# The memory values' panel first, the keys scaled as they are evicted, twelve zero products

## The chip, the cores and the metric

The kernel runs on one core of a Trainium2 chip. The metric is the time of one execution on the device, in microseconds. Of the core's engines, TensorE (PE in the profile) multiplies, VectorE (DVE) and ScalarE (ACT) work element by element and empty the accumulators, GpSimd (POOL) only sets a few constants, and SyncE (SP) issues nearly all transfers.

## What is computed

A trunk of two layers over 256 tokens of width 2048. Layer 0 mixes with gated linear attention, layer 1 with forgetting attention; each layer also attends with 4 heads to 256 memory tokens, and each ends in a gated MLP with a short convolution. The change touches how the memory's keys and values come about. The reference for that part:

```python
def memory_kv(mem_n, w_kv):
    mk, mv = split_cols(mem_n @ w_kv, [MEM_WIDTH, MEM_WIDTH])
    return split_heads(mk, MEM_HEADS), split_heads(mv, MEM_HEADS)
...
    mem_n = rmsnorm(mem, norm_mem)
...
    for i in range(DEPTH):
...
        mk, mv = memory_kv(mem_n, mem_w_kv[i])
```

MEM_WIDTH is 512: keys and values of a layer are 256 tokens by 512 columns, from weights of 2048 rows. rmsnorm divides each token by the root of the mean of its squares and multiplies by a gain for each of the 2048 columns.

## The kernel before

All weights are one stream (`wp`), laid out by `_panels` (L55) in the order in which they are used. A panel is one group of output columns over all 16 chunks of 128 rows. It is cut into units of 512 KB, 128 x 1024 numbers: four chunks of 256 columns, or two chunks of 512.

Every product is made from parts, to keep float32 accuracy. `load_unit` and `split_unit` (L187 to L211) load a unit into `raw` (four buffers), cast it on ScalarE to its high part `whi` (three buffers, L201) and subtract on VectorE to get its low part `wlo` (L210). They run at a raised priority, up to 300 instructions ahead of where they stand. `split` (L302 to L310) does the same to a chunk of activations: the high half of a buffer is cast with the gain on ScalarE (L309), the low half computed on VectorE (L310). `bufA` and `bufB` hold 16 such chunks each.

There are two kinds of panel:

- `proj_fm` (L213) leaves the output with its columns on the partitions. The weights are the stationary side, the activations (high and low side by side, 512 columns) the moving one: for each chunk and each of two accumulators a product of 512 columns with `whi` (L235) and one of 256 with `wlo` (L236). A panel has 4 units. `whole` (L240) adds an accumulator's two halves.
- `proj_tm` (L248) leaves the tokens on the partitions. The activations are stationary, the weights (up to 512 columns) move: for each chunk and each of two blocks of tokens three products (L272 to L274). A panel has 8 units of two chunks; in each unit block 0 goes first.

Both take two of the four accumulators (`acc`, pool `pacc`) for a panel and empty them when the panel is over, with the function `evac` that they are given.

The start of the run goes like this. Eight zero products (`WARM`, L177 and L178) of 128 x 512 keep TensorE busy from a cleared buffer. Then come two keys' panels of layer 0 (`("mk", 0, j)`, 256 columns each, `proj_fm`), its values' panel (`("mv", 0)`, 512 columns, `proj_tm`), and the same three for layer 1. The memory itself comes in during the first panel: `take_mem` (L431) is called ahead of each half of a unit, issues the transfers of `memt` (first tile in two pieces, one on ScalarE's queue, then a tile of 512 KB for each unit) and splits two chunks into `bufA`. The transfers of `gains`, `mask`, `xf` (the input, 16 pieces) and `x` are issued on SP's queue between those of the weights; `tc.issue_after` holds them behind a named instruction.

The memory's norm (`Norm`, L312, here `nrm`) isn't applied to the activations, only the gain is; the factor of each token is applied to the outputs. In `first_out` (L466), after the first panel, four squares are taken (L473) and added up (L475 to L477). `mean` (L329) sums over the partitions with small products against ones (L334); `col` (L347) makes the factor of each token as a column on the partitions, with Newton steps on VectorE (L342 to L345); `row` (L358) turns it into a row with two more products (L370) and a copy (L373). The values take the column as they are evicted (`mv_out`, L464). The keys of layer 0 are evicted without the norm (L453, L454) and all four tiles of them are multiplied by the row when the second panel is over (L457); those of layer 1 are multiplied by the row as they are evicted (L459).

The order of the instructions on each engine is set when the kernel is built, by a scheduler that goes by priorities and by its own estimate of when each is ready; each engine then runs its list in order. The scheduler isn't changed.

Of the kernel before, what the change touches and what calls it, by code (L numbers as in the profile page):

```python
# [12 lines left out]
F32 = mybir.dt.float32  # L13
# [6 lines left out]
P = 128  # L20
# [18 lines left out]
AHEAD = 300  # L39

OG_EARLY = 2
WARM = 8

FV_PARTS = ((0, 376), (376, 764), (764, 1152), (1152, 1536))

# [9 lines left out]
def _panels():  # L55

    full = list(range(KC))
    out = []  # L60

    def fm(key, w, c0, kcs=full, second=None):
        cols = [(c0, 256)] if second is None else [(c0, 128), (second, 128)]
        out.append((key, w, kcs, cols, 4))

    def tm(key, w, c0, n, kcs=full, more=()):
        out.append((key, w, kcs, [(c0, n), *more], 2))

    for l in range(2):
        for j in range(2):  # L70
            fm(("mk", l, j), ("mem_w_kv", l), j * 256)
        tm(("mv", l), ("mem_w_kv", l), 512, 512)
    tm(("gv", 0), ("gla_w_in", 0), G_V, DV, more=[(G_R, RANK)])
    for j in range(2):
        fm(("mq", 0, j), ("gla_w_in", 0), G_MQ + j * 256)
    for h in range(GLA_H):
        fm(("gq", h), ("gla_w_in", 0), G_Q + h * DK)
        fm(("gk", h), ("gla_w_in", 0), G_K + h * DK)
        for j in range(OG_EARLY if h == GLA_H - 1 else 0):
            fm(("og", j), ("gla_w_in", 0), G_OG + j * 256)  # L80
# [12 lines left out]

    for f in range(4):
        tm(("wo", 0, f), ("gla_w_out", 0), f * 512, 512, late)
    ffn(0)
    for j in range(6):
        fm(("fk", j), ("fox_w_kv", None), F_K + j * 256)
    for j, (lo, hi) in enumerate(FV_PARTS):
        more = [] if j else [(F_L, FOX_H)]  # L100
        tm(("fv", j), ("fox_w_kv", None), F_V + lo, hi - lo, more=more)
    for j in range(2):
        fm(("mq", 1, j), ("fox_w_in", 0), FOX_H * HD + j * 256)
    for j in range(6):
        fm(("fq", j), ("fox_w_in", 0), j * 256)
    for f in range(4):
        tm(("wo", 1, f), ("fox_w_out", 0), f * 512, 512, late)
    ffn(1)
    return out
# [29 lines left out]
def _trunk(ctx: ExitStack, tc: tile.TileContext, xt, xtok, memt, wp, wgu, gns, gfin, cnv, par, msk, out):  # L139
# [70 lines left out]
                V.tensor_tensor(lo[:, s], raw[:, s], hi[:, s].bitcast(F32), ALU.subtract)  # L210
        return hi, lo  # L211

    def proj_fm(key, src, evac, before=None):  # L213

        units = where[key]
        total = sum(len(u[1]) for u in units)
        acc = [pacc.tile([P, 512], F32, name="acc", tag="acc") for _ in range(2)]
        base = min(min(u[1]) for u in units)
        done = 0
        for n, unit in enumerate(units):  # L220
            if before is None:
                hi, lo = split_unit(unit)
            else:
                hi, lo = split_unit(unit, 2, lambda half: before(n, half), whole=n > 0)
            for j, kc in enumerate(unit[1]):
                for c in range(2):
                    product(acc[c], c, total - 1, done, src[kc - base], hi, lo, j)
                done += 1
        for c in range(2):
            evac(c, acc[c])  # L230
# [14 lines left out]
        V.tensor_tensor(r, a[:, :T], t, ALU.add)  # L245
        return r

    def proj_tm(key, src, evac, spare=None):  # L248

        units = where[key]
        n = units[0][2]
        base = min(min(u[1]) for u in units)
        acc = [pacc.tile([P, 512], F32, name="acc", tag="acc") for _ in range(2)]
        ahead = 0 if spare is None else 4
        ready = {}
        for i in range(len(units) + ahead):
            for b, u in ((0, i), (1, i - ahead)):
                if not 0 <= u < len(units):  # L260
                    continue
                if b == 0:
                    ready[u] = split_unit(units[u], pool=wpool if spare is None or u < 3 else spare)
                hi, lo = ready[u]
                kcs = units[u][1]
                a = acc[b][:, :n]
                xs = slice(b * P, (b + 1) * P)
                for j, kc in enumerate(kcs):
                    s = slice(j * n, (j + 1) * n)
                    xk = src[kc - base]  # L270
                    last = u == len(units) - 1 and j == len(kcs) - 1
                    TE.matmul(a, xk[:, 0, xs], hi[:, s], start=u == 0 and j == 0, stop=False)  # L272
                    TE.matmul(a, xk[:, 0, xs], lo[:, s], start=False, stop=False)  # L273
                    TE.matmul(a, xk[:, 1, xs], hi[:, s], start=False, stop=last)  # L274
                if u == len(units) - 1:
                    evac(b, a)
# [150 lines left out]
    with tc.tile_pool(name="load", bufs=1) as lp:  # L427
        mraw = [lp.tile([P, KC + 4 * T], F32, name=f"mt{i}") for i in range(4)]
        mt = [t[:, KC:].rearrange("p (c t) -> p c t", t=T) for t in mraw]

        def take_mem(g, half):  # L431

            if g == 0:
                s = slice(half * (KC + 2 * T), KC + (half + 1) * 2 * T)
                (nc.sync if half else nc.scalar).dma_start(mraw[0][:, s], memt[0, :, s])
                if half == 0:
                    S.preload_act_table_set("natural_log_exp_and_others")
                chunks = range(2 * half, 2 * half + 2)
            else:
                if half == 0:  # L440
                    nc.sync.dma_start(mraw[g][:, KC:], memt[g, :, KC:])
                    if g == 1:
                        nc.sync.dma_start(gains, gns)
                chunks = range(2 * half, 2 * half + 2)
            for i in chunks:
                k = 4 * g + i
                split(bufA, k, mt[g][:, i, :], mraw[0][:, k : k + 1])

        def mk_out(l, j):
            def evac(c, a):  # L450
                o = mk[l][:, 2 * j + c, :]
                if l == 0:
                    S.activation(o, a[:, T:], AF.Copy)  # L453
                    V.tensor_tensor(o, o, a[:, :T], ALU.add)  # L454
                    if c == 1 and j == 1:
                        for f in range(MEM_H):
                            V.tensor_tensor(mk[0][:, f, :], mk[0][:, f, :], nrm.row(), ALU.mult)  # L457
                else:
                    V.tensor_tensor(o, whole(a), nrm.row(), ALU.mult)  # L459

            return evac

        def mv_out(l):
            return lambda b, a: S.activation(mv[l][:, b, :], a, AF.Copy, scale=nrm.col()[:, b : b + 1])  # L464

        def first_out(c, a):  # L466
            mk_out(0, 0)(c, a)
            if c == 1:
                nc.sync.dma_start(mask[:, :M_FOX], msk[:, :M_FOX])
                sq, acc = [lp.tile([P, 4, T], F32, name=n) for n in ("sq4", "ssq4")]  # L470
                with tc.issue_after(casts[-1].ins):
                    for g in range(4):
                        S.activation(sq if g else acc, mt[g], AF.Square)  # L473
                        if g:
                            V.tensor_tensor(acc, acc, sq, ALU.add)  # L475
                V.tensor_tensor(acc[:, :2, :], acc[:, :2, :], acc[:, 2:, :], ALU.add)
                V.tensor_tensor(acc[:, 0, :], acc[:, 0, :], acc[:, 1, :], ALU.add)  # L477
                nrm.acc = acc[:, 0, :]

        proj_fm(("mk", 0, 0), bufA, first_out, before=take_mem)  # L480
        proj_fm(("mk", 0, 1), bufA, mk_out(0, 1))
        xf = [lp.tile([P, T], F32, name=f"xf{i}") for i in range(KC)]
        with tc.issue_after(loads[-1].ins):
            for i in range(KC):
                nc.sync.dma_start(xf[i], xt[i])
            nc.sync.dma_start(part, par)
            nc.sync.dma_start(mask[:, M_FOX:], msk[:, M_FOX:])
        proj_tm(("mv", 0), bufA, mv_out(0))
        for i in range(KC):
            split(bufB, i, xf[i], gain("mix0", i))  # L490
        for j in range(2):
            proj_fm(("mk", 1, j), bufA, mk_out(1, j))
            if j == 0:
                with tc.issue_after(loads[-1].ins):
                    for f in range(4):
                        nc.sync.dma_start(x[f], xtok[f])
                for f in range(4):
                    for b in range(2):
                        nx.add(f, b)
        proj_tm(("mv", 1), bufA, mv_out(1))  # L500


# [482 lines left out]
```

## Time and profile before

| | |
|---|---|
| median of 3 runs | 2298.16 us (2298.02 to 2298.43) |
| the profiled execution's own time | 2298.03 us |
| its span in the trace | 2296.2 us |
| TensorE busy | 2284.1 us |
| VectorE busy | 1619.1 us |
| ScalarE busy | 1253.6 us |
| granted TensorE clock, mean | 0.999 |

The span runs from the first to the last recorded instruction; 1.83 us of the execution lie outside it. A row of the timeline has the start and the length in microseconds, the engine, the line of the kernel, the operation, what is written and read with its shape, how many instructions were merged, and in brackets how long the engine was idle before and what ended that. Products on TensorE are pipelined: their lengths overlap, and the distance between starts is what each one costs. A row of the waits has who waited for whom, the total in microseconds, the times, and the longest. A row of the stretches has the borders, the length, then busy time and instructions of PE, its weight loads (PEld), DVE, ACT and POOL, the granted clock, the share of the transfers' engines, and GB/s. A row of the transfers has what is loaded, the queue, the count, the size and the median time from issue to landing. A row of a tile's view has the shortest, the median and the longest in nanoseconds, the first and last start, and the shape.

### The profile page before, as it was taken

The page shows a single profiled execution, that of the slowest core. Times are in us where ns is not written, and L with a number is a line of the kernel's source. Part 1 is how long each engine was busy: PE and PEld are TensorE (multiplying, and loading weights), DVE is VectorE, ACT ScalarE, POOL GpSimd, SP SyncE. Part 2 cuts the span into 40 slices and gives each one's busy share as a digit, 9 for nine tenths or more (in the row PEclk, how much of TensorE's full clock was granted, in tenths as well). Part 3 has the DMA queues.
Part 4 walks back from the last instruction along what each step waited for, and adds up shares of the span by engine and source line. Part 5 has one row for each costly group of instructions (what it writes and reads, how often), then busy time and mean ns, then how long its engine had stood idle before and what let it go on. Part 6 is the DMA issues. An engine that isn't in the chain of part 4 may idle for free.

```text
span 2296.2 us, 33165 instructions
## 1 busy us (share of the span) xinstructions
PE 2284.1 (99%) x12384; PEld 1976.2 (86%) x12384; DVE 1619.1 (71%) x2667; ACT 1253.6 (55%) x1967; POOL 3.1 (0%) x20
## 2 busy tenths in 40 slices
PE   9999999999999999999999999999999999999998
PEld 7889888888888888888888998888888888888886
DVE  7578987577765777557767557657776577756775
ACT  7555555555553555445565455556554455534554
POOL 0000000000000000000000000000000000000000
PEclk9999999999999999999999999999999999999999
DMA  8655455555555555555555664555555555665554
GB/s 320 196 162 161 156 164 179 187 184 189 190 189 194 188 191 187 193 192 191 186 183 187 182 194 152 170 193 184 188 189 192 192 191 186 191 193 192 185 192 156
DMA packets 124745, 430.15 MB, mean 187 GB/s; under 512 B 14108, under 2 KB 18600, under 8 KB 124456
## 3 DMA queue, kind: packets, MB, share of 16 engines
q1 hardware_dynamic: 124152, 427.24, 57.3%
q8 instruction: 97, 1.59, 0.3%
q10 hardware_dynamic: 432, 0.79, 0.1%
q14 instruction: 64, 0.52, 0.1%
HBM read 425.87 MB, written 2.11 MB: 186 GB/s over the span
## 4 chain that ended last, share of the span: by engine, by line
PE 99%; DMA 0%; DVE 0%; ACT 0%; issue 0%; DVEq 0%; ACTq 0%; SPq 0%
PE acc L235 37%; PE acc L236 20%; PE acc L273 12%; PE acc L274 12%; PE acc L272 12%; PE acc L238 2%; PE ps_s L842 0%; PE ps_s L631 0%; PE ps_t L402 0%; PE ps_s L409 0%; PE ps_o L420 0%; PE ps_s L756 0%; PE ps_o L772 0%; PE ps_o L650 0%; DMA raw<-wp 0%; DMA cb<-cdram 0%
## 5 line engine op out<-in xcount | busy, mean ns | idle before, releaser
L210 DVE TENSOR_TENSOR wlo<-raw,whi 128x1024 fp32r<-128x1024 f32 (+4 forms) x812 | 972.8, 1199 | 542.3 <-ACT whi L201 531.3
L201 ACT ACTIVATE whi<-raw 128x1024 fp32r<-128x1024 f32 (+4 forms) x812 | 843.5, 1040 | 778.4 <-PE acc L274 373.7
L235 PE MATMUL acc<-B,whi 128*128 128x512 f32 x1980 | 683.6, 395 | 0.0
L235 PE MATMUL acc<-A,whi 128*128 128x512 f32 x1680 | 580.9, 397 | 1.3 <-DVE A L310 1.3
L236 PE MATMUL acc<-B,wlo 128*128 128x256 f32 x2112 | 550.0, 281 | 0.0
L236 PE MATMUL acc<-A,wlo 128*128 128x256 f32 x1792 | 464.0, 281 | 0.0
L235 PEld LDWEIGHTS acc<-B,whi 128*128 128x128 f32 x1980 | 360.7, 188 | 68.5
L236 PEld LDWEIGHTS acc<-B,wlo 128*128 128x128 f32 x2112 | 397.4, 188 | 21.9
L235 PEld LDWEIGHTS acc<-A,whi 128*128 128x128 f32 x1680 | 305.7, 188 | 58.7 <-DVE A L310 2.0
L236 PEld LDWEIGHTS acc<-A,wlo 128*128 128x128 f32 x1792 | 338.3, 189 | 20.2
L273 PE MATMUL acc<-wlo,B 128*128 128x512 f32 (+3 forms) x736 | 274.8, 374 | 0.9 <-DVE wlo L210 0.9
L274 PE MATMUL acc<-whi,B 128*128 128x512 f32 (+3 forms) x736 | 273.6, 372 | 0.0
L272 PE MATMUL acc<-whi,B 128*128 128x512 f32 (+3 forms) x736 | 247.2, 372 | 0.0
L273 PE MATMUL acc<-wlo,A 128*128 128x512 f32 x544 | 212.3, 390 | 0.0
L274 PE MATMUL acc<-whi,A 128*128 128x512 f32 x544 | 211.8, 389 | 0.0
L272 PE MATMUL acc<-whi,A 128*128 128x512 f32 x544 | 192.4, 390 | 0.0
L243 ACT ACTIVATE part<-acc 128x256 f32<-128x256 f32 x240 | 89.9, 375 | 156.7 <-PE acc L238 156.6
L273 PEld LDWEIGHTS acc<-wlo,B 128*128 128x128 f32 x736 | 138.2, 188 | 20.5 <-DVE wlo L210 1.2
L274 PEld LDWEIGHTS acc<-whi,B 128*128 128x128 f32 x736 | 138.2, 188 | 18.6
L272 PEld LDWEIGHTS acc<-whi,B 128*128 128x128 f32 x736 | 137.3, 188 | 18.7
L245 DVE TENSOR_TENSOR wholes<-acc,part 128x256 f32<-128x256 f32 x240 | 101.2, 422 | 64.2 <-ACT part L243 63.9
L274 PEld LDWEIGHTS acc<-whi,A 128*128 128x128 f32 x544 | 102.2, 188 | 21.1
(213 smaller groups left out, 1578.5 us busy)
## 6 DMA issues: line engine op xcount, KB each, us to landing
raw<-wp SPq DMA_DIRECT2D x743, 512.0 KB, 3.4
raw<-wp SPq DMA_DIRECT2D x32, 384.0 KB, 3.1
raw<-wp SPq DMA_DIRECT2D x24, 388.0 KB, 3.1
raw<-wp SPq DMA_DIRECT2D x8, 400.0 KB, 3.1
xf<-xt SPq DMA_DIRECT2D x16, 128.0 KB, 4.4
x<-xtok SPq DMA_DIRECT2D x4, 512.0 KB, 7.5
mt<-memt SPq DMA_DIRECT2D x3, 512.0 KB, 6.8
cb<-cdram SPq DMA_DIRECT2D x12, 128.0 KB, 3.2
```

What stands on the lines that cost most here:

```text
L201: casts.append(S.activation(hi[:, s], raw[:, s], AF.Copy))
L210: V.tensor_tensor(lo[:, s], raw[:, s], hi[:, s].bitcast(F32), ALU.subtract)
L235: TE.matmul(a, hi[:, s], both, start=done == 0, stop=False)
L236: TE.matmul(a[:, :T], lo[:, s], both[:, 0, :], start=False, stop=False)
L238: TE.matmul(a, hi[:, s], both, start=False, stop=True)
L243: S.activation(t, a[:, T:], AF.Copy)
L245: V.tensor_tensor(r, a[:, :T], t, ALU.add)
L272: TE.matmul(a, xk[:, 0, xs], hi[:, s], start=u == 0 and j == 0, stop=False)
L273: TE.matmul(a, xk[:, 0, xs], lo[:, s], start=False, stop=False)
L274: TE.matmul(a, xk[:, 1, xs], hi[:, s], start=False, stop=last)
```

## The change

Layer 0's values' panel is laid out and computed first, its two keys' panels follow; layer 1 keeps its order. `take_mem` now serves `proj_tm`: each unit takes two chunks, and a 512 KB tile of the memory is fetched with every second unit. The squares are taken one tile at a time inside that panel, the last at its end; the norm's column is made for the values' eviction at the end of the first panel, and the row for the keys' eviction, which now multiplies as layer 1's does. The transfers of `mask` and `gains` are issued after the first panel's last load, those of `xf` after the first keys' panel's last load. The zero products are twelve.

```diff
-WARM = 8
+WARM = 12
...
     for l in range(2):
+        if l == 0:
+            tm(("mv", l), ("mem_w_kv", l), 512, 512)
         for j in range(2):
             fm(("mk", l, j), ("mem_w_kv", l), j * 256)
-        tm(("mv", l), ("mem_w_kv", l), 512, 512)
+        if l:
+            tm(("mv", l), ("mem_w_kv", l), 512, 512)
...
-    def proj_tm(key, src, evac, spare=None):
+    def proj_tm(key, src, evac, spare=None, before=None):
...
-                    ready[u] = split_unit(units[u], pool=wpool if spare is None or u < 3 else spare)
+                    pool = wpool if spare is None or u < 3 else spare
+                    if before is None:
+                        ready[u] = split_unit(units[u], pool=pool)
+                    else:
+                        ready[u] = split_unit(units[u], 2, lambda half: before(u, half), pool, whole=u > 0)
...
+        def take_mem(u, half):
+
+            if half == 0:
+                if u == 0:
+                    nc.scalar.dma_start(mraw[0][:, :n0], memt[0, :, :n0])
                     S.preload_act_table_set("natural_log_exp_and_others")
+                elif u == 1:
+                    nc.sync.dma_start(mraw[0][:, n0:], memt[0, :, n0:])
+                elif u % 2 == 0:
+                    nc.sync.dma_start(mraw[u // 2][:, KC:], memt[u // 2, :, KC:])
+            k = 2 * u + half
+            split(bufA, k, mt[k // 4][:, k % 4, :], mraw[0][:, k : k + 1])
+            if half and u in (3, 5, 7):
+                square(u // 2 - 1)
+
+        n0 = KC + 2 * T
+        sq, ssq = [lp.tile([P, 4, T], F32, name=n) for n in ("sq4", "ssq4")]
+
+        def square(g):
+            S.activation(sq if g else ssq, mt[g], AF.Square)
+            if g:
+                V.tensor_tensor(ssq, ssq, sq, ALU.add)
 
         def mk_out(l, j):
             def evac(c, a):
                 o = mk[l][:, 2 * j + c, :]
-                if l == 0:
-                    S.activation(o, a[:, T:], AF.Copy)
-                    V.tensor_tensor(o, o, a[:, :T], ALU.add)
-                    if c == 1 and j == 1:
-                        for f in range(MEM_H):
-                            V.tensor_tensor(mk[0][:, f, :], mk[0][:, f, :], nrm.row(), ALU.mult)
-                else:
-                    V.tensor_tensor(o, whole(a), nrm.row(), ALU.mult)
+                V.tensor_tensor(o, whole(a), nrm.row(), ALU.mult)
...
+        def first_out(b, a):
+            if b == 0:
+                square(3)
+                V.tensor_tensor(ssq[:, :2, :], ssq[:, :2, :], ssq[:, 2:, :], ALU.add)
+                V.tensor_tensor(ssq[:, 0, :], ssq[:, 0, :], ssq[:, 1, :], ALU.add)
+                nrm.acc = ssq[:, 0, :]
+                with tc.issue_after(loads[-1].ins):
+                    nc.sync.dma_start(mask[:, :M_FOX], msk[:, :M_FOX])
+                    nc.sync.dma_start(gains, gns)
+            mv_out(0)(b, a)
+
+        proj_tm(("mv", 0), bufA, first_out, before=take_mem)
         xf = [lp.tile([P, T], F32, name=f"xf{i}") for i in range(KC)]
...
+        for l in range(2):
+            for j in range(2):
+                proj_fm(("mk", l, j), bufA, mk_out(l, j))
+                if l == j == 0:
+                    with tc.issue_after(loads[-1].ins):
+                        for i in range(KC):
+                            nc.sync.dma_start(xf[i], xt[i])
+                        nc.sync.dma_start(part, par)
+                        nc.sync.dma_start(mask[:, M_FOX:], msk[:, M_FOX:])
+                elif j == 0:
+                    with tc.issue_after(loads[-1].ins):
+                        for f in range(4):
+                            nc.sync.dma_start(x[f], xtok[f])
                     for f in range(4):
-                        nc.sync.dma_start(x[f], xtok[f])
...
+                        for b in range(2):
+                            nx.add(f, b)
+            if l == 0:
+                for i in range(KC):
+                    split(bufB, i, xf[i], gain("mix0", i))
         proj_tm(("mv", 1), bufA, mv_out(1))
```

More of the change, by code (lines that the diff above doesn't have):

```diff
@@ L211, in split_unit, with proj_fm @@
         return hi, lo
-    def proj_fm(key, src, evac, before=None):
+    def proj_fm(key, src, evac):
         units = where[key]
@@ L220, in proj_fm @@
         for n, unit in enumerate(units):
-            if before is None:
-                hi, lo = split_unit(unit)
-            else:
-                hi, lo = split_unit(unit, 2, lambda half: before(n, half), whole=n > 0)
+            hi, lo = split_unit(unit)
             for j, kc in enumerate(unit[1]):
@@ L429, in _trunk @@
         mt = [t[:, KC:].rearrange("p (c t) -> p c t", t=T) for t in mraw]
[L431 to L436, printed above, removed]
-                    S.preload_act_table_set("natural_log_exp_and_others")
[L438 to L447, printed above, removed]
+        def take_mem(u, half):
+            if half == 0:
+                if u == 0:
+                    nc.scalar.dma_start(mraw[0][:, :n0], memt[0, :, :n0])
+                    S.preload_act_table_set("natural_log_exp_and_others")
+                elif u == 1:
[12 more added lines that the diff above has]
+                V.tensor_tensor(ssq, ssq, sq, ALU.add)
         def mk_out(l, j):
@@ L451, in evac @@
                 o = mk[l][:, 2 * j + c, :]
-                if l == 0:
-                    S.activation(o, a[:, T:], AF.Copy)
-                    V.tensor_tensor(o, o, a[:, :T], ALU.add)
-                    if c == 1 and j == 1:
-                        for f in range(MEM_H):
-                            V.tensor_tensor(mk[0][:, f, :], mk[0][:, f, :], nrm.row(), ALU.mult)
-                else:
-                    V.tensor_tensor(o, whole(a), nrm.row(), ALU.mult)
+                V.tensor_tensor(o, whole(a), nrm.row(), ALU.mult)
             return evac
@@ L464, in mv_out @@
             return lambda b, a: S.activation(mv[l][:, b, :], a, AF.Copy, scale=nrm.col()[:, b : b + 1])
[L466 to L478, printed above, removed]
@@ L480, in _trunk @@
-        proj_fm(("mk", 0, 0), bufA, first_out, before=take_mem)
-        proj_fm(("mk", 0, 1), bufA, mk_out(0, 1))
-        xf = [lp.tile([P, T], F32, name=f"xf{i}") for i in range(KC)]
[L483 to L494, printed above, removed]
-                    for f in range(4):
-                        nc.sync.dma_start(x[f], xtok[f])
-                for f in range(4):
-                    for b in range(2):
-                        nx.add(f, b)
+        def first_out(b, a):
[8 more added lines that the diff above has]
+            mv_out(0)(b, a)
```

## The prediction

> **What bounds the kernel now.** I began with the page, then the waits of TensorE, then the first 60 us of the timeline, engine by engine, because only there does the change move anything.
>
> ```profile
> span 2296.2 us, 33165 instructions
> ...
> PE 2284.1 (99%) x12384; PEld 1976.2 (86%) x12384; DVE 1619.1 (71%) x2667; ACT 1253.6 (55%) x1967; POOL 3.1 (0%) x20
> ...
> PE 99%; DMA 0%; DVE 0%; ACT 0%; issue 0%; DVEq 0%; ACTq 0%; SPq 0%
> ```
>
> ```profile
> PE ps_o L178 <- DVE B L175: 1.4, 1, 1.4
> PE acc L235 <- DVE A L310: 1.3, 1, 1.3
> PE acc L273 <- DVE wlo L210: 0.9, 1, 0.9
> ```
>
> TensorE (PE) is the bound from its first instruction to the last product. In the whole span it waits three times: 1.4 us before the zero products, 1.3 us between them and the first real product, 0.9 us once much later. The change keeps every real product, so PE's work has a floor that it cannot lower. What can move is the start, and any wait that the new order brings in.
>
> ```profile
> 1.45 3.78 PE L178 MATMUL ps_o<-B 128*128 128x512 f32 x8 [1.45 <-DVE B L175]
> 6.54 0.80 PE L235 MATMUL acc<-A,whi 128*128 128x512 f32 x1 [1.32 <-DVE A L310]
> ...
> 7.78 0.41 PE L236 MATMUL acc<-A,wlo 128*128 128x256 f32 x1
> ...
> 8.42 0.41 PE L236 MATMUL acc<-A,wlo 128*128 128x256 f32 x1
> ...
> 9.70 0.53 PE L235 MATMUL acc<-A,whi 128*128 128x512 f32 x1
> 10.07 0.40 PE L236 MATMUL acc<-A,wlo 128*128 128x256 f32 x2
> ...
> 10.54 0.28 PE L236 MATMUL acc<-A,wlo 128*128 128x256 f32 x1
> ...
> 10.89 0.27 PE L236 MATMUL acc<-A,wlo 128*128 128x256 f32 x1
> ...
> 19.44 0.63 PE L235 MATMUL acc<-A,whi 128*128 128x512 f32 x2
> ...
> 30.68 0.62 PE L272 MATMUL acc<-whi,A 128*128 128x512 f32 x2
> ...
> 33.41 0.62 PE L272 MATMUL acc<-whi,A 128*128 128x512 f32 x2
> ```
>
> These are starts and lengths on PE. A pair of a 512- and a 256-column product comes every 0.64 us at first (7.78 to 8.42) and every 0.35 us later (10.54 to 10.89); the step between the paces lies between 9.70 and 10.07, say 9.9 us, 3.4 us after the real work began. So 512 columns cost 0.64 x 512/768 = 0.427 us at the slow pace. The first keys' panel takes 19.44 - 6.54 = 12.90 us, the second, with the same products, 30.68 - 19.44 = 11.24 us. The slow pace costs 1.66 us. That sum is the most a better warm-up can return, apart from an earlier start.
>
> **The change, part by part.** Zero products: 12 instead of 8. At 0.427 us each PE is free for other work at 1.45 + 12 x 0.427 = 6.57 us if the pace stays slow until then. (Eight by this working are free at 4.87; the row ends at 5.23 because it includes the last one's way through the array.) Today the real work starts at 6.54, so the four additional ones fill the hole of 1.32 us and delay the start by 0.03 us. What is new is that PE is busy without a break from 1.45 us on.
>
> When the pace rises is the one unknown. In the trace a busy stretch of 3.78 us and a hole did not raise it, and a second stretch raised it after 3.4 us. If 3.4 us of unbroken work are what is wanted, the earliest time is 1.45 + 3.4 = 4.85. With the same reading and the same rhythm as in the trace (steps possible at 9.9, 6.5 and 3.1 us) it rises at 6.5, just as the zero products end. I take 6.5: all of the 1.66 us is then saved. At 4.85, eight zero products are through, and four more at 0.23 us end at 5.8: the real work could start 0.7 us earlier too. At the other end the gain from the pace is nil.
>
> The Trainium skill, page "TensorE: Matmul & The Clock Gate", section "Part 1: The HAM clock gate", says that PE starts at half rate and goes to full rate after a free-running window of about 3.4 us in which it was busy, the window's phase being different from run to run. By that rule the step falls somewhere between 4.9 and 8.3 us here, and the saving between 0.8 and 2.4 us. The trace's 3.4 us and its two paces agree; that eight products failed in one profile fits a window that began before them. The same rule speaks against counting on an exact figure.
>
> The values' panel first: can the first products be fed? The rows are landings of DMAs, two issues on SP's queue, the rate of one stretch, then ScalarE (ACT) and VectorE (DVE).
>
> ```profile
> raw<-wp SPq DMA_DIRECT2D x2, 256.0 KB, 4.2
> mt<-memt ACTq DMA_DIRECT2D x1, 264.0 KB, 4.2
> ...
> 1.18 0.42 SPq L435 DMA_DIRECT2D mt<-memt  x1
> 1.65 0.42 SPq L198 DMA_DIRECT2D raw<-wp  x1
> ...
> 5.00:10.00 5.00, 3.68 (x11) 2.98 (x11) 4.60 (x11) 5.00 (x12) 0.00 (x0) 1.00 1.04 419
> ```
>
> ```profile
> 4.74 0.63 ACT L201 ACTIVATE whi<-raw 128x512 fp32r<-128x512 f32 x1 [2.29 <-DMA raw<-wp]
> 5.27 1.69 ACT L309 ACTIVATE A<-mt 128x256 fp32r<-128x256 f32 x4
> ...
> 8.99 1.14 ACT L201 ACTIVATE whi<-raw 128x512 fp32r<-128x512 f32 x2
> 10.03 1.71 ACT L309 ACTIVATE A<-mt,mt 128x256 fp32r<-128x256 f32 x4
> ...
> 5.40 0.69 DVE L210 TENSOR_TENSOR wlo<-raw,whi 128x512 fp32r<-128x512 f32 x1 [4.01 <-ACT whi L201]
> 6.01 1.67 DVE L310 SCALAR_TENSOR_TENSOR A<-mt,A 128x256 fp32r<-128x256 f32 x4
> 9.78 1.29 DVE L210 TENSOR_TENSOR wlo<-raw,whi 128x512 fp32r<-128x512 f32 x2
> 10.98 1.67 DVE L310 SCALAR_TENSOR_TENSOR A<-mt,mt,A 128x256 fp32r<-128x256 f32 x4
> ```
>
> One unit of weights (512 KB) feeds PE for 33.41 - 30.68 = 2.73 us in the values' panel and 8 x 0.35 = 2.8 us in a keys' panel, but it asks for two chunks of the memory instead of four. ACT then needs 1.04 + 2 x 0.40 = 1.84 us a unit where it now needs 2.65, DVE 1.20 + 2 x 0.40 = 2.0 instead of 2.8. So today both engines run exactly as fast as PE in the first panel; afterwards they have 0.7 to 0.9 us a unit to spare. That matters because PE at full pace asks for unit 1 earlier than now.
>
> The transfers: up to unit 2 they are 264 + 3 x 256 + 3 x 512 = 2568 KB; 520 KB of it is there at 4.74, the rest follows at 419 GB/s in 2.10 MB / 0.419 = 5.0 us, at 9.75 us. PE wants unit 2 at 6.57 + 2 x 2.73 = 12.0; a half cast, a chunk's split and the low parts take 0.63 + 0.49 + 0.69 + 0.48 = 2.3 us in a row, so it is met even then. Unit 1 (1544 KB, 7.2 us, wanted at 9.3) is as safe, and units 3 to 7 need 1024 and 512 KB in turn per 2.73 us. The second half of unit 0 is the closest: the half lands near 5.9 at the latest (issued at 1.65 as now, + 4.2; in the new order it takes the place at 1.18), its cast follows by 6.5 and its low part by 7.3, and PE wants them at 6.57 + 3 x 0.23 = 7.3. I cost that at 0, bounded by 0.4 us. A first product that no longer spans a chunk's high and low half can go at 5.27 + 0.49 = 5.8; with 12 zero products at slow pace that gives nothing.
>
> The norm of the memory and the evictions:
>
> ```profile
> 15.32 1.04 ACT L473 ACTIVATE ssq<-mt 128x1024 f32<-128x1024 f32 x1
> ...
> 17.35 1.22 DVE L475 TENSOR_TENSOR ssq<-ssq,sq 128x1024 f32<-128x1024 f32 x1 [0.71 <-ACT sq L473]
> ...
> 34.71 0.42 DVE L477 TENSOR_TENSOR ssq<-ssq 128x256 f32<-128x256 f32 x1
> 36.59 0.61 PE L334 MATMUL ps_t<-mask,ssq 128*128 128x128 f32 x4
> ...
> 45.51 0.16 DVE L345 TENSOR_TENSOR ny<-ny,nt 128x2 f32<-128x2 f32 x1
> ...
> 51.98 0.69 ACT L464 ACTIVATE mv<-acc,ny 128x512 f32<-128x512 f32 x1 [0.53 <-PE acc L274]
> 54.58 0.36 ACT L373 ACTIVATE row<-ps_t 128x256 f32<-128x256 f32 x1
> L457 DVE TENSOR_TENSOR mk<-mk,row x4: 418/418/426, 55.0 to 56.0; 128x256 f32<-128x256 f32 x4
> L459 DVE TENSOR_TENSOR mk<-wholes,row x4: 424/424/427, 66.1 to 78.5; 128x256 f32<-128x256 f32 x4
> ```
>
> Four multiplications of 0.418 us go and four of 0.424 come, and copies and additions keep their number: nothing on PE. The four squares (1.04 us) and three additions (1.22 us) move forward into the first panel, into the spare time above: three squares are 3 us against 8 x 0.9 = 7 us on ACT. The DMAs of mask and gains move behind the eight units' weights on SP's queue; the first use of the mask is the product of L334. The 16 of xf move to behind the first keys' panel, still two panels into the run; what is made of them is read only after layer 1's three memory panels.
>
> New is a wait. There are four accumulators. Values' and first keys' panel take them all; the second keys' panel needs those of the values, whose eviction needs the column ny, and layer 1's keys need those of the first, whose eviction needs the row. In the new order the values end at 6.57 + 8 x 2.73 = 28.4, the first keys at 28.4 + 11.24 = 39.7, the second at 50.9. The column comes today 45.67 - 34.71 = 11.0 us after the start of the last addition, the row 20.2 us after it. The last square needs the last memory transfer (with the weights ahead of it 5128 KB: 4.74 + 4.72 MB / 0.419 = 16 us, later if the weights' buffers hold it back); then ACT's spare time sets it near 20 to 22, DVE's last addition near 25. Column at 36, eviction at 37; row at 45, evictions at 47. Both are 3 to 4 us ahead of need. Behind a late eviction stand ACT's and DVE's casts of the next units. Price 0, if the last addition starts by 28.
>
> Sum against the profiled execution: 2298.03 us, of which 1.83 lie outside its span; +0.03 - 1.66 + 0 = 2296.4. The runs' median is 2298.16, 0.13 above that execution, so 2296.5 us.
>
> **Rivals.** First, the pace rises later. If it takes 3.4 us of slow zero work plus 3.4 us of slow real work, counted together from 1.45, it rises near 1.45 + 3.8 + 3.4 = 8.6; 2.0 us at slow pace after 6.57 cost 1.0, the gain is 0.6, the time 2297.5. For it: eight products were not enough. Against: a hole lay in between.
>
> Second, the change doesn't do what it says: products of zeros do not count, and the pace rises 3.4 us after the real start, at 9.97. Then the cost is today's plus 0.03: 2298.2. For it: 3.78 us of them had no visible effect.
>
> Third, slower: the late column. If the last square queues on ACT behind the casts until the values' panel is over, it ends at 29.4, the additions (1.22, 0.69, 0.42) with a unit's low part between them (1.22) start their last by 32.6, the column comes at 43.6, the eviction ends at 44.3, and PE stands from 39.7 on: 4.6 us, and up to 1.66 again if a hole of that length brings the slow pace of the start back. 2298.16 - 1.63 + 4.6 + 1.66 = 2302.8. It decides as soon as the last addition starts after 28. For it: today the chain is loose, 11 and 20 us for a few small operations. Against: ACT has spare time before 28, and nothing else wants it.
>
> **How the numbers follow.** Forecast 0.68, later rise 0.14, no effect 0.08, late column 0.10 (half of it a partial stall of 1 to 3 us, so 2297.5 to 2299.5). The forecast's own range is 2295.8 (pace up at 4.85) to 2297.4 (up one step of 3.4 us after that, at 8.3, so (8.3 - 6.57)/2 = 0.9 us lost). The range runs from 2295.2, with 0.5 us for an earlier start than the sum allows, to 2299.0, which takes in the two mild rivals and most partial stalls. About 0.2%, 4.6 us, is what a measurement tells from no change: faster by that 0.02 (nothing found could give it), slower 0.04 (the full late column, or a stall that I do not see), within it 0.94.
>
> **What would show it.** Right: twelve zero products from 1.45 us, no hole of a microsecond after them, pairs of products 0.23 us apart from the first or second unit on, no wait of PE on an accumulator near 40 or 51 us, and the start of layer 1's keys 1.6 us earlier than today. Wrong: 0.427 us a product beyond 9 us (the first two rivals), a wait on a low part or a chunk in the first 15 us (the feed was mis-sized), or idle PE near 40 us with the eviction of the values behind it (the third).

## The result, and the profile after

| | median of 11 runs | range | ratio to before (95%) |
|---|---|---|---|
| before | 2298.16 us | 2298.01 to 2298.73 | |
| after | 2303.95 us | 2301.80 to 2305.68 | 1.0025 [1.0017, 1.0032] |

The change makes the kernel slower by 5.8 us, where a gain of 1.7 us was forecast. The executions also scatter: over 3.9 us, where those of the kernel before scatter over 0.7. The profiled execution of after is the fastest of the eleven (2301.80 us, span 2299.7). A second execution is shown among the experiments.

The page of the kernel after, and its waits of TensorE. In the code after, L181 is the line of the zero products, L204 and L213 make a unit's high and low part, L276 to L278 are the three products of a values' panel, L313 and L314 split a chunk, L454 and L456 are the squares and their additions, L466 evicts the values.

```profile
span 2299.7 us, 33177 instructions
...
PE 2285.0 (99%) x12388; PEld 1976.1 (86%) x12388; DVE 1618.6 (70%) x2671; ACT 1253.9 (55%) x1971; POOL 3.1 (0%) x20
```

```profile
PE acc L277 <- DVE wlo L213: 2.4, 3, 0.9
PE acc L235 <- DVE wholes L245: 2.1, 1, 2.1
PE ps_o L181 <- DVE B L178: 1.4, 1, 1.4
PE acc L276 <- ACT whi L204: 0.2, 1, 0.2
```

TensorE's busy time is nearly what it was. New are a wait of 2.1 us for `wholes`, which is the emptying of a keys' accumulator, and waits for casts and low parts (of the three for low parts one comes late in the run and was there before, too). The timeline of TensorE after, at the places that matter:

```profile
1.45 5.36 PE L181 MATMUL ps_o<-B 128*128 128x512 f32 x12 [1.45 <-DVE B L178]
6.65 0.62 PE L276 MATMUL acc<-whi,A 128*128 128x512 f32 x2
...
12.52 0.73 PE L276 MATMUL acc<-whi,A 128*128 128x512 f32 x2 [0.23 <-ACT whi L204]
13.87 0.50 PE L277 MATMUL acc<-wlo,A 128*128 128x512 f32 x1 [0.61 <-DVE wlo L213]
...
20.57 0.50 PE L277 MATMUL acc<-wlo,A 128*128 128x512 f32 x1 [0.93 <-DVE wlo L213]
...
31.16 0.40 PE L235 MATMUL acc<-A,whi 128*128 128x512 f32 x1
...
45.16 0.50 PE L235 MATMUL acc<-A,whi 128*128 128x512 f32 x1 [2.13 <-DVE wholes L245]
...
56.80 0.62 PE L235 MATMUL acc<-A,whi 128*128 128x512 f32 x2
```

The panels begin at 6.65 (values), 31.16 (first keys), 45.16 (second keys) and 56.80 us (layer 1's keys). The last point was reached at 53.17 us before. That is 3.6 us later, and the span grew by 3.5: all of the loss lies ahead of this point, and what follows is unchanged. The values' panel took 24.51 us instead of 8 x 2.73 = 21.8: 2.7 us lost. The first keys' panel and the hole behind it took 14.00 us, where the panel alone needs 11.24 and the norm's small products 0.4: 2.4 us lost. The two losses, less the 1.66 us of the slow pace that are gone, come to 3.4 us.

Who stood ahead? The timelines of ScalarE and VectorE after:

```profile
7.31 1.04 ACT L454 ACTIVATE ssq<-mt 128x1024 f32<-128x1024 f32 x1
8.26 1.14 ACT L204 ACTIVATE whi<-raw 128x512 fp32r<-128x512 f32 x2
...
10.90 1.05 ACT L454 ACTIVATE sq<-mt 128x1024 f32<-128x1024 f32 x1
11.86 2.17 ACT L204 ACTIVATE whi<-raw 128x512 fp32r<-128x512 f32 x4
...
46.41 1.27 ACT L466 ACTIVATE mv<-acc,ny 128x512 f32<-128x512 f32 x2 [1.96 <-DVE ny L349]
```

```profile
11.98 1.23 DVE L456 TENSOR_TENSOR ssq<-ssq,sq 128x1024 f32<-128x1024 f32 x1 [0.20 <-ACT sq L454]
13.13 2.49 DVE L213 TENSOR_TENSOR wlo<-raw,whi 128x512 fp32r<-128x512 f32 x4
...
26.39 0.41 DVE L472 TENSOR_TENSOR ssq<-ssq 128x256 f32<-128x256 f32 x1
...
33.29 0.15 DVE L340 TENSOR_SCALAR nv<-ps_t 128x2 f32<-128x2 f32 x1
...
39.23 0.87 DVE L314 SCALAR_TENSOR_TENSOR B<-xf,gains,B 128x256 fp32r<-128x256 f32 x2
...
44.70 0.41 DVE L245 TENSOR_TENSOR wholes<-acc,part 128x256 f32<-128x256 f32 x1
...
46.23 0.15 DVE L349 TENSOR_TENSOR ny<-ny,nt 128x2 f32<-128x2 f32 x1
```

Two squares run before the casts of unit 2 (the casts of L204 at 11.86), though the code calls the first of them in unit 3; an addition of 1.23 us runs before the unit's low part at 13.13. That is the first loss. The scheduler put them there by its own estimate of what is ready when; why that estimate has the units' data so late was not tried. The last addition starts at 26.39, but the column (`ny`) is done only at 46.4, 20.0 us later; the first of the chain's small steps on VectorE (`nv`) is at 33.29, and between them stand low parts and splits of `xf` (the row at 39.23 holds two of the sixteen). So at 42.9, when the first keys' panel is over, all four accumulators are full, and TensorE waits until one of the keys' is emptied at 45.1. Even that emptying is late: the copy on ScalarE is done at 43.24, the addition on VectorE (44.70) stands behind a low part and more splits of `xf`.

### The profile page after: what moved, and what is told of

The parts are those of the page before. It is cut to its first block, busy times and chain, and to the rows that moved or that the text cites. A ratio compares the mean times of both kernels' runs of the same rounds, so it can differ in the third digit from the quotient of the medians.

```text
span 2299.7 us, 33177 instructions
## 1 busy us (share of the span) xinstructions
PE 2285.0 (99%) x12388; PEld 1976.1 (86%) x12388; DVE 1618.6 (70%) x2671; ACT 1253.9 (55%) x1971; POOL 3.1 (0%) x20
## 4 chain that ended last, share of the span: by engine, by line
PE 97%; DVE 1%; DMA 1%; ACT 1%; issue 0%; DVEq 0%; SPq 0%; ACTq 0%
PE acc L235 37%; PE acc L236 20%; PE acc L277 12%; PE acc L276 12%; PE acc L278 12%; PE acc L238 2%; PE ps_s L842 0%; PE ps_s L631 0%; DMA xf<-xt 0%; DVE wlo L213 0%; PE ps_t L406 0%; PE ps_s L413 0%; PE ps_o L424 0%; PE ps_s L756 0%; PE ps_o L772 0%
## 5 line engine op out<-in xcount | busy, mean ns | idle before, releaser
L213 DVE TENSOR_TENSOR wlo<-raw,whi 128x1024 fp32r<-128x1024 f32 (+3 forms) x816 | 972.6, 1193 | 545.9 <-ACT whi L204 533.6
L204 ACT ACTIVATE whi<-raw 128x1024 fp32r<-128x1024 f32 (+3 forms) x816 | 843.6, 1035 | 777.7 <-PE acc L278 372.0
L278 PE MATMUL acc<-whi,B 128*128 128x512 f32 (+3 forms) x736 | 273.6, 372 | 0.0
L276 PE MATMUL acc<-whi,B 128*128 128x512 f32 (+3 forms) x736 | 247.3, 372 | 0.0
L278 PE MATMUL acc<-whi,A 128*128 128x512 f32 x544 | 211.6, 389 | 0.0
L276 PE MATMUL acc<-whi,A 128*128 128x512 f32 x544 | 192.2, 391 | 0.2 <-ACT whi L204 0.2
L278 PEld LDWEIGHTS acc<-whi,B 128*128 128x128 f32 x736 | 138.3, 188 | 18.7
L276 PEld LDWEIGHTS acc<-whi,B 128*128 128x128 f32 x736 | 137.3, 188 | 18.7
L277 PEld LDWEIGHTS acc<-wlo,A 128*128 128x128 f32 x544 | 102.1, 188 | 23.5 <-DVE wlo L213 2.4
```

Source lines behind the costliest of these rows:

```text
L204: casts.append(S.activation(hi[:, s], raw[:, s], AF.Copy))
```

## The experiments

Medians stand beside those of the kernel before on the same chip, 2298.41 us (33 runs, 2297.93 to 2299.36) for the first four and 2298.37 (27 runs) for the next three.

**Twelve zero products in the kernel before.** What is the warm-up worth by itself?

```diff
-WARM = 8
+WARM = 12
```

> The kernel before with twelve zero products, nothing else of the change. If the warm-up does what the forecast says (pace of 0.23 us per 512 columns from the first real product on), the slow pace of 1.66 us goes: 2296.5 us, and a keys' first panel of 11.3 us instead of 12.9. If the start gains nothing, or the longer warm-up delays the first product by more than it saves: 2298.2 or more.

Measured: 2298.31 us (2298.01 to 2298.83, 11 runs), ratio 0.9999 [0.9990, 1.0008]. No gain: the time is that of the second case expected, though the pace of the first is there. Its timeline of TensorE, and what ran on ScalarE and VectorE ahead of the low part at 20.11:

```profile
6.60 0.50 PE L235 MATMUL acc<-A,whi 128*128 128x512 f32 x1 [0.42 <-DVE A L310]
...
9.97 0.73 PE L235 MATMUL acc<-A,whi 128*128 128x512 f32 x2 [0.28 <-ACT whi L201]
...
20.11 0.51 PE L236 MATMUL acc<-A,wlo 128*128 128x256 f32 x2 [0.72 <-DVE wlo L210]
...
30.94 0.63 PE L272 MATMUL acc<-whi,A 128*128 128x512 f32 x2
```

```profile
15.67 1.04 ACT L473 ACTIVATE ssq<-mt 128x1024 f32<-128x1024 f32 x1
16.62 1.04 ACT L473 ACTIVATE sq<-mt 128x1024 f32<-128x1024 f32 x1
17.56 1.99 ACT L201 ACTIVATE whi<-raw 128x1024 fp32r<-128x1024 f32 x2
...
17.69 1.22 DVE L475 TENSOR_TENSOR ssq<-ssq,sq 128x1024 f32<-128x1024 f32 x1 [0.87 <-ACT sq L473]
18.84 2.35 DVE L210 TENSOR_TENSOR wlo<-raw,whi 128x1024 fp32r<-128x1024 f32 x2
```

The products go at full pace from the first, and TensorE then waits for the cast and the low part, waits that the slow pace used to hide. The second keys' panel begins at 18.77 us, so each of the two panels takes 12.17 us where 11.24 would do. The first is held by the splits, which leave both engines next to no idle time there. The second is held at its first low part, and ahead of that unit's cast and low part stand two squares and an addition of the norm. The two panels end at 30.94 us, against 30.68 with eight. So the slow pace of the old order cost nothing: it lay over a feed that was no faster. Whether twelve would pay there with the squares out of the way was not tried.

**The squares held back** (`squares_held`). Each square and its addition go behind the cast that was issued last:

```diff
         def square(g):
-            S.activation(sq if g else ssq, mt[g], AF.Square)
-            if g:
-                V.tensor_tensor(ssq, ssq, sq, ALU.add)
+            with tc.issue_after(casts[-1].ins):
+                S.activation(sq if g else ssq, mt[g], AF.Square)
+                if g:
+                    V.tensor_tensor(ssq, ssq, sq, ALU.add)
```

> The change, with each square held behind the cast that was issued last, so that it can't go ahead of the casts of units 1 and 2. Theory of the feed: TensorE's waits for casts and low parts before 21 us (0.23 + 0.61 + 0.93 us in the trace, 2.7 us of the panel's length) come from squares and their additions ahead of them; they go, the first panel takes 21.8 to 22.5 us instead of 24.5. As the last addition then starts some 3 us later, theory of the column expects the wait near 43 us to grow by what the panel gave back, so a median between 2301 and 2304. If the feed is short for another reason (transfers, the splits' own order), the first panel stays at 24 us or more.

Measured: 2303.60 us (2301.81 to 2304.22), ratio 1.0021 [1.0012, 1.0029]. TensorE and one stretch of the table of stretches:

```profile
6.37 0.63 PE L276 MATMUL acc<-whi,A 128*128 128x512 f32 x2
...
28.61 0.62 PE L235 MATMUL acc<-A,whi 128*128 128x512 f32 x2
...
43.42 0.77 PE L235 MATMUL acc<-A,whi 128*128 128x512 f32 x1 [2.94 <-DVE wholes L245]
```

```profile
43.40:47.00 3.60, 3.58 (x11) 3.10 (x12) 2.54 (x10) 0.00 (x0) 1.71 (x5) 0.53 0.96 250
```

The values' panel takes 28.61 - 6.37 = 22.24 us: 2.3 us less than in after, and no wait in it. So the waits of the first panel came from the squares. But the hole ahead of the second keys' panel grows to 2.94 us, and behind it the granted clock is 0.53 for 3.6 us. What one end gave back the other took, though not as the theory of the column had it: the hole grew by 0.8 us only, and the slow pace took the other 1.5 (the second keys' panel takes 13.16 us, 11.64 in after).

**The accumulators freed from the column.** The values are copied out unscaled, then multiplied in place:

```diff
-            return lambda b, a: S.activation(mv[l][:, b, :], a, AF.Copy, scale=nrm.col()[:, b : b + 1])
+            def evac(b, a):
+                if l == 0:
+                    S.activation(mv[0][:, b, :], a, AF.Copy)
+                    a = mv[0][:, b, :]
+                S.activation(mv[l][:, b, :], a, AF.Copy, scale=nrm.col()[:, b : b + 1])
+
+            return evac
```

> The change, with the values copied out of their accumulators unscaled and multiplied by the column afterwards in place, so that the accumulators no longer wait for the column. Theory of the column: the wait of 2.1 us before the second keys' panel goes, median near 2301.5, with the waits of the first panel unchanged. Theory of the feed alone: the median stays within 0.7 us of 2304.

Measured: 2300.18 us (2299.28 to 2301.29), ratio 1.0007 [0.9998, 1.0016]; 3.8 us less than after, more than the 2.1 us of the wait, and 1.3 us below what was expected. ScalarE and TensorE:

```profile
32.92 0.57 ACT L468 ACTIVATE mv<-acc 128x512 f32<-128x512 f32 x1
...
47.28 1.34 ACT L470 ACTIVATE mv<-mv,ny 128x512 f32<-128x512 f32 x2 [0.65 <-DVE ny L349]
...
42.70 0.63 PE L235 MATMUL acc<-A,whi 128*128 128x512 f32 x2
```

The accumulators are emptied at 32.92 and 34.34, the column still comes after 47, and nobody minds: the second keys' panel begins at 42.70, right behind the first. The waits of the first panel are unchanged (0.20, 0.61 and 0.99 us).

**The input one panel later** (`input_later`). Why is the column late?

```diff
-                if l == j == 0:
+                if l == 0 and j == 1:
                     with tc.issue_after(loads[-1].ins):
                         for i in range(KC):
                             nc.sync.dma_start(xf[i], xt[i])
...
                 elif j == 0:
                     with tc.issue_after(loads[-1].ins):
                         for f in range(4):
                             nc.sync.dma_start(x[f], xtok[f])
```

> The change, with the 16 transfers of xf issued after the second keys' panel's loads instead of the first's. Why is the column late? If the splits of xf stand between the Newton steps on VectorE (column 20 us after the last addition, 11 us before), the column comes near 40 us, the values are evicted before the first keys' panel ends, and the wait of 2.1 us near 43 us goes: median near 2301.5. If the chain is slow by itself (low parts, small products placed late), the wait stays and the median is near 2304.

The edit does more than that. The branch below it (`elif j == 0`) now runs for layer 0 as well, so the four transfers of `x` are issued twice, the first time from 26.8 us on, and ScalarE takes 16 squares more (92 against 76 on its line). `part` and the rest of the mask move along with `xf`.

Measured: 2299.77 us (2299.24 to 2300.27), ratio 1.0005 [0.9996, 1.0014]. VectorE and ScalarE:

```profile
37.38 0.16 DVE L349 TENSOR_TENSOR ny<-ny,nt 128x2 f32<-128x2 f32 x1
...
38.77 1.25 ACT L466 ACTIVATE mv<-acc,ny 128x512 f32<-128x512 f32 x2
```

The last addition starts at 26.28, as in after, and the column is done at 37.5: 11.3 us, close to the 11.0 of the kernel before. From 31.9 us, where the chain's first step on VectorE starts, to its end only low parts stand between the steps. Without the splits of `xf` the chain has its old length, and the eviction at 38.77 is in time. So the splits made it late. The median is 4.2 us below after, 1.7 us lower than expected, in spite of the additional work.

**Both cures.** Squares held, values copied out unscaled (`held_unscaled`).

> The change with both cures: squares held behind the last cast, values copied out unscaled. If feed and column are the only two losses of the change, TensorE has no wait of more than 0.5 us between the zero products and 60 us, the first panel takes 22.2 us as with the squares held, the second keys' panel follows the first at once, and the median is 2300.2 - 2.3 = 297.9 at most, 2296.5 to 2298 us, below the kernel before. If something else of the change costs as well (a third wait that these two hid), it stays above 2298.4.

(The difference in the first number should read 2297.9.) Measured: 2297.02 us (2296.59 to 2298.26), ratio 0.9994 [0.9986, 1.0003]. TensorE:

```profile
28.71 0.62 PE L235 MATMUL acc<-A,whi 128*128 128x512 f32 x2
...
40.42 0.62 PE L235 MATMUL acc<-A,whi 128*128 128x512 f32 x2
...
51.74 0.62 PE L235 MATMUL acc<-A,whi 128*128 128x512 f32 x2
```

No wait between the zero products and 60 us; layer 1's keys begin at 51.74 us, 1.4 us earlier than in the kernel before. The median is 1.35 us under that kernel's. The interval still holds 1, though most of it lies below, so a gain over that kernel is likely but not shown. Feed and column were the two losses of the change: with both cured, TensorE has no third wait in the first 60 us.

**Squares held and input later** instead:

> The change with squares held and the input's transfers one panel later, values scaled as they are evicted. The column can start only after the last square, 3 us later than in input_later, so it comes near 43 us, just where the second keys' panel wants the accumulators. Theory of the column: a short wait of 0 to 2 us near 40 us is left, median 2297 to 2299.5. If the splits of xf were all that made it late: no wait, same time as held_unscaled within 0.5 us.

Measured: 2297.18 us (2296.66 to 2297.99), ratio 0.9995 [0.9986, 1.0003]. The column was in time after all (values evicted at 38.70), since its chain shortened to 9.5 us; no wait was left near 40 us, and the two cures are worth the same, though this one carries the additional transfers and squares of `input_later`.

**Both cures with eight zero products:**

> The same as held_unscaled with eight zero products. If the values' panel first is what lets the warm-up pay (its units ask for half the memory's chunks), the eight lose most of the 1.66 us that the slow pace costs: 1.0 to 1.8 us above held_unscaled, and the first products 0.427 us apart for some 3.4 us. If the warm-up pays nothing here either, as in the old order: within 0.5 us.

Measured: 2297.13 us (2296.57 to 2298.53), ratio 0.9995 [0.9986, 1.0004]: 0.11 us above the twelve, far within the scatter. Yet its trace goes at the slow pace from 5.95 to about 9.6 us, and layer 1's keys begin at 52.43 us, 0.7 later than with twelve. The four executions at the end are about this: each was run once, for the place of the step between the paces.

**The changed kernel again.**

> The changed kernel itself once more, for a second trace: its first trace was of the fastest of 11 executions (2301.8), most take 2303 to 2305. Theory of the pace: the additional 1 to 3 us are a stretch at the slow pace after one of the waits, seen as products of 512 columns 0.43 us apart after 20 or 45 us and a granted clock below 1 there. Rival: longer waits for transfers, with the pace unchanged.

Measured: 2304.92 us. TensorE, VectorE and a stretch:

```profile
46.23 0.50 PE L235 MATMUL acc<-A,whi 128*128 128x512 f32 x1 [3.15 <-DVE wholes L245]
...
47.73 0.63 PE L235 MATMUL acc<-A,whi 128*128 128x512 f32 x1
48.15 0.41 PE L236 MATMUL acc<-A,wlo 128*128 128x256 f32 x1
48.37 0.63 PE L235 MATMUL acc<-A,whi 128*128 128x512 f32 x1
...
50.68 0.40 PE L235 MATMUL acc<-A,whi 128*128 128x512 f32 x1
```

```profile
46.20:50.30 4.10, 4.07 (x15) 3.50 (x16) 3.12 (x9) 1.69 (x3) 1.63 (x5) 0.59 0.75 244
```

Both theories have a part. The wait is 1.0 us longer than in the first trace (there ScalarE had gone to the full accumulator at 42.88, here only at 44.15, behind splits that had waited for transfers of `xf`). And the hole is now long enough that the slow pace follows: pairs 0.64 us apart until 50.3, a granted clock of 0.59, 1.5 us more in that panel (13.11 against 11.64). Together they are 2.5 us, of 3.1 between the two spans (2302.8 and 2299.7); the rest is a longer wait for a low part late in the run (1.46 us at 1318.23, 0.88 in the first trace).

**The place of the step**, in four more executions:

> held_unscaled_warm8 once more, for the place of the step in the pace. If the step comes a fixed 3.4 us after the real work's start, it is again near 9.5 us and the trace is 0.7 to 1.0 us longer than held_unscaled's. If its place changes from execution to execution, it lies elsewhere between 5 and 9.5 us, which would explain medians only 0.1 us apart.

> held_unscaled_warm8, a third look. Fixed place of the step: near 9.5 us again. Changing place: elsewhere between 5 and 9.5 us, and the time moves with it.

> held_unscaled once more. Fixed place: the zero products end at 6.7 to 6.9 us again. Changing place: they end anywhere from 6.1 to 7.0 us, at 0.43 us apiece before the step and 0.23 after it, and the real work starts between 5.9 and 6.7.

> The kernel before once more. Fixed place: step near 9.9 us. Changing place: elsewhere; and if the first panel is held by its feed anyway, the second keys' panel starts near 19.4 us (18.8 with twelve zero products and no slow pace) wherever the step lies.

The place changes from execution to execution. With the cures and eight zero products the step came near 9.6 us, near 10.4 and, in the third execution, before the first real product. With the cures and twelve the real work began at 6.71 us the first time and at 5.94 the second. The kernel before, whose first trace had the step at 9.9 us, shows this in the second:

```profile
1.45 3.57 PE L178 MATMUL ps_o<-B 128*128 128x512 f32 x8 [1.45 <-DVE B L175]
6.49 0.50 PE L235 MATMUL acc<-A,whi 128*128 128x512 f32 x1 [1.48 <-DVE A L310]
6.83 0.28 PE L236 MATMUL acc<-A,wlo 128*128 128x256 f32 x1
6.94 0.39 PE L235 MATMUL acc<-A,whi 128*128 128x512 f32 x1
...
30.66 0.63 PE L272 MATMUL acc<-whi,A 128*128 128x512 f32 x2
```

Eight were enough that time, the first pairs are 0.35 us apart or little more, and the two panels end at 30.66 us: 0.02 us from where they ended at the slow pace. This is the experiment on the 1.66 us that the forecast rested on, made by the chip itself. One expectation was missed: the second keys' panel began at 18.52 us, not near 19.4. The first panel did gain 0.9 us, and the second lost it, most of it in a wait of 0.67 us for its first low part (until 19.82), the one behind the norm's squares.

With the cures the pace does count. Layer 1's keys begin at 52.43 and 52.73 us where eight products were not enough, and at 51.41 where they were; with twelve they begin at 51.74 and 51.90. In all of the nine traces with twelve, cured or not, the real work began at full pace, or was there within its first products; it began between 5.94 and 6.74 us.

The four executions took 2298.24, 2298.93, 2296.91 and 2298.28 us; one of the kernel before beside them, without a trace, took 2300.88. The third with eight, the earliest at layer 1's keys, is slow for another reason: a wait for a low part at 1310 us, 0.8 to 1.25 us in the other cured traces, took 1.80 here, and from 1311.7 to 1315.1 the products came at half the pace (granted clock 0.61 from 1310.8 to 1315.1):

```profile
1310.85 0.45 PE L277 MATMUL acc<-wlo,B 128*128 128x388 f32 x1 [1.80 <-DVE wlo L213]
```

## Why the prediction was wrong

Wrong in the sign and in the size: 2296.5 us forecast, 2303.95 measured. What failed are two terms that the sum put at 0, steps 2 and 3 below; step 4 adds to them.

1. **"That sum is the most a better warm-up can return"**, the 1.66 us of the slow pace. This term did not make the kernel slower. The pace came as forecast, full from 6.65 us on, and that it rose near the 6.5 taken is in part luck, since the place changes. In the old order the sum was not to be had: two panels end at 30.66 to 30.94 us at either pace. The prediction had seen that ScalarE and VectorE "run exactly as fast as PE in the first panel", and did not draw the consequence that a faster TensorE would wait there. In the new order nearly all of it was: with both cures layer 1's keys begin 1.43 us earlier than before, and the median is 1.35 us lower.

2. **"Three squares are 3 us against 8 x 0.9 = 7 us on ACT"**: a mean over the panel where the place decides. The spare time arises late in the panel (ScalarE has no idle time of note before 22 us), the squares ran early, two of them ahead of unit 2's casts at 11.86 us. The wait fell where the cover was thinnest: unit 2 was wanted at 12.0. Priced at 0, it measured 2.7 us over the panel's 21.8; `squares_held` takes 2.3 of them away and every wait of that panel.

3. **"Price 0, if the last addition starts by 28."** It started at 26.39 and the price was 2.4 us in one trace and 3.4 in the other. The 11.0 us from the last addition to the column were taken from a stretch in which the splits of `xf` were nearly over; the change puts them between the steps of that chain, and it took 20.0 us. The working for the 16 transfers, "what is made of them is read only after layer 1's three memory panels", answered when their results are wanted, but not what their splits would stand in front of. `input_later` shows it by giving the chain its 11 us back. The third rival had the wait on the late column right, but not its reason: it had the column late because the last square was, and that came in time (20.17 us on ScalarE). That its 2302.8 us lies near the measured time is luck.

4. **The pace after a hole** stood in the rival only. It fits the scatter of the executions: the hole is 2.1 us in the fast trace, without a fall, and 2.9 and 3.2 us in two others (`squares_held`, and the changed kernel again), with a fall that lasts about 3.5 us and costs 1.5. The recorded mean clocks agree: of the eleven executions of after, the four at 0.997 or 0.998 took 2304.54 us or more, of the seven at 0.999 only one did. It would also explain why removing a wait of 2.1 to 3.2 us brought 3.8 us; with two traces of the changed kernel that is argued, not shown.

The transfers' working held: TensorE waited for no transfer in the first panel, and the values' panel alone took 22.2 us with the squares out of the way. That no product is saved on TensorE held as well. The chance of 0.04 for slower by over 0.2% was far too low for a change with two new waits on an engine that is busy 99% of its span.

## What to carry to other kernels

Before a stretch at a low clock is counted as a loss, ask whether the engine would be fed at the full one: the rows of the engines that feed it say so, if they have no idle time either. A chain of small steps has no length of its own on an engine with an ordered list; it takes as long as what is put between its steps, so its duration from another moment of the run doesn't carry over to a new place. And an accumulator that waits for a late factor is better emptied unscaled: two more copies off the critical engine (0.57 us of ScalarE each here) took the chain out of the path.

## What the hardware showed

The step of TensorE's pace is not tied to the work. Eight zero products, a row of 3.5 to 3.8 us, raised it before the real work in 2 of 5 traces; 12 did in all nine, or within the first products. The Trainium skill, page "TensorE: Matmul & The Clock Gate", section "Part 1: The HAM clock gate", gives a free-running window of about 3.4 us as the reason, and the traces agree: 3.8 us of work hold a whole window only when it happens to fall well. The three late steps (9.6, 9.9 and 10.4 us), less 3.4, fall at 6.2 to 7.0 us, when eight products were over and twelve, or the real ones right behind them, still ran.

How long a hole may be, these runs do not settle. After 1.69 us (`squares_held`, at 1315 us) and 2.13 us the pace stayed; after 1.80, 2.94 and 3.15 us it fell, at once or within 0.9 us of the products' new start, and came back 3.4 to 3.6 us after the fall. The Trainium skill's advice on the same page, section "Why this matters for your kernels", to leave no gap of more than about 3 us between bursts of products, is too loose where 1.80 us was enough; the measurement decides.

The granted clock shows the fall after a hole (0.53, 0.59 and 0.61) but not the slow pace at the start of the run: the row of 5 to 10 us of the kernel before says 1.00 while its products came at half the pace. There only the distance between products tells.
